# A row softmax on one core: part of a load moved to the store queue, and scaling row by row

## The chip, the cores and the metric

The kernel runs on one core of a Trainium2 chip. The time is that of the device, in microseconds, from the start to the end of one execution; lower is better. The core has several engines that work at the same time, each through its own list of instructions in order: VectorE (DVE), ScalarE (ACT), GpSimd (POOL) and SyncE (SP). TensorE (PE) has nothing to do here. Data goes between HBM and the on-chip memory SBUF through 16 DMA engines. A transfer is issued by SP, ScalarE or GpSimd; each of these has a queue of its own on the 16 engines (in the profile q1 is SP's, q10 is ScalarE's, q0 is GpSimd's).

## The reference

```python
def reference(x: np.ndarray) -> np.ndarray:      # x: 16 x 1024 x 512, float32
    temp = 0.5
    x_scaled = x / temp
    x_max = np.max(x_scaled, axis=-1, keepdims=True)
    exp_x = np.exp(x_scaled - x_max)
    return (exp_x / np.sum(exp_x, axis=-1, keepdims=True)).astype(np.float32)
```

It is a softmax over rows of 512 numbers, 16,384 rows. Input and output are 33.55 MB each.

## The kernel before

**Tiling.** The rows are cut into 8 chunks. A chunk is 128 partitions x 16 rows x 512 numbers, 4 MB; a partition holds 16 rows that follow each other in memory, so a whole chunk is 128 contiguous pieces of 32 KB. There are six buffers (`BUFS`), each for one chunk, and all work on a chunk is done in place: chunk 6 takes the buffer of chunk 0, chunk 7 that of chunk 1. `LOADS`, `BLOCKS` and `STORES` (L38 to L40) say in which groups of rows a chunk is loaded, worked on and stored. Chunk 0 is loaded as rows 0 to 3 and rows 4 to 15 and worked on in three blocks (4, 4 and 8 rows); chunks 1 to 6 are loaded and worked on whole; chunk 7 is loaded without its last row and worked on in two blocks of 8. Every chunk is stored whole. In all there are 11 blocks.

**The steps of a block.**

- `shift` (L71) issues the load of the chunk on SP when the chunk is new (L68), takes the maximum of each row, negated, on VectorE (L77, a reduce), and doubles it into a bias (L81).
- `exponentials` (L102) runs on ScalarE, one instruction for each row (L108): exp(2x + bias), with the sum of the row as a second result, which shows in the profile as an instruction of its own, ACTIVATION_READ_ACCUMULATOR.
- `scale_vector` (L120) takes the reciprocals of the sums on VectorE (L125) and multiplies seven eighths of the block's rows with them in one instruction (L127), whose second operand is the reciprocal spread over the row.
- `scale_scalar` (L133) multiplies the last eighth of the rows on ScalarE, one instruction for each (L138): two rows of 16, one of 8, none of 4.
- `store` (L144) issues the store of the whole chunk on ScalarE's queue behind the chunk's last block (L148).

**Order.** The order on each engine is that of the program text; a transfer or an instruction that needs another's result waits for it on its engine, and what stands behind it on that engine waits too. The loop over the blocks (L163) goes one block ahead with the exponentials and two ahead with the reduces:

```python
    exponentials(0, rows(0)[0])
    for i in range(n):
        if i + 1 < n:
            exponentials(i + 1, rows(i + 1)[0])
        scale_vector(i)
        scale_scalar(i)
        if i + 2 < n:
            shift(i + 2)
        store(i)
        if i + 1 < n:
            exponentials(i + 1, rows(i + 1)[1])
```

`rows` (L157) splits a block's exponentials into a part ahead of the store and a part behind it. Only chunk 1 has a second part, its last two rows (L159): the store of chunk 0 is issued after 14 of the 16 exponentials of chunk 1.

**Transfers.** SP issues the loads of chunks 0 to 5 at the start, without waiting. Its load of chunk 6 waits for the store of chunk 0 to land, that of chunk 7 for the store of chunk 1. The last row of chunk 7 is loaded by GpSimd (`load_last_row`, L88), in small pieces, after the eleventh exponential of chunk 5 has given the sign (L116). ScalarE's queue carries the eight stores and nothing else.

Of the kernel before, what the change touches and what calls it, by code (L numbers as in the profile page):

```python
# [1 line left out]

# [4 lines left out]


@with_exitstack
def kernel(  # L10
    ctx: ExitStack,
    tc: tile.TileContext,
    x: bass.AP,
    out: bass.AP,
):
    nc = tc.nc
    fp32 = mybir.dt.float32
    P = nc.NUM_PARTITIONS
    AX = mybir.AxisListType.X
    EXP = mybir.ActivationFunctionType.Exp  # L20
    COPY = mybir.ActivationFunctionType.Copy
    MAX = mybir.AluOpType.max

    D = x.shape[-1]
    xf = x.flatten_outer_dims()
    of = out.flatten_outer_dims()
    N = xf.shape[0]

    G = 16
    C = N // (P * G)
    assert C * P * G == N
    xr = xf.rearrange("(c p g) d -> c p g d", p=P, g=G)
    outr = of.rearrange("(c p g) d -> c p g d", p=P, g=G)
    WHOLE = [(0, G)]
    LOADS = [[(0, 4), (4, G)]] + [WHOLE] * 6 + [[(0, G - 1)]]  # L38
    BLOCKS = [[(0, 4), (4, 8), (8, G)]] + [WHOLE] * 6 + [[(0, 8), (8, G)]]
    STORES = [WHOLE] * 8  # L40
    BMAX = 16
    BUFS = 6

    data = ctx.enter_context(tc.tile_pool(name="data", bufs=BUFS))
    stats = ctx.enter_context(tc.tile_pool(name="stats", bufs=6))

    ctx.enter_context(tc.manual_schedule())


    warm = stats.tile([P, 1], fp32, name="warm", bufs=1)  # L50
    nc.vector.memset(warm, 0.0)  # L51
    nc.scalar.activation(out=warm, in_=warm, func=EXP)  # L52

    chunks = {}
    blocks = [(c, lo, hi) for c in range(C) for lo, hi in BLOCKS[c]]
    n = len(blocks)
    biases, sums, recips = {}, {}, {}

    finished = []

    def load(c):
        if c < BUFS:
            chunks[c] = data.tile([P, G, D], fp32, name="xt")
        else:
            chunks[c] = chunks[c - BUFS]
        xt = chunks[c]
        for lo, hi in LOADS[c]:
            part = nc.sync.dma_start(out=xt[:, lo:hi, :], in_=xr[c][:, lo:hi, :])  # L68
            finished.append(part.ins.name)

    def shift(i):  # L71
        c, lo, hi = blocks[i]
        if c not in chunks:
            load(c)
        b = hi - lo
        negmax = stats.tile([P, BMAX], fp32, name="negmax")
        nc.vector.tensor_reduce(  # L77
            negmax[:, 0:b], chunks[c][:, lo:hi, :], axis=AX, op=MAX, negate=True
        )
        biases[i] = stats.tile([P, BMAX], fp32, name="bias")  # L80
        nc.vector.tensor_scalar_mul(biases[i][:, 0:b], negmax[:, 0:b], 2.0)  # L81

    def load_last_row(signal):  # L88
        seen = stats.tile([P, 1], fp32, name="seen", bufs=1)
        copied = nc.gpsimd.tensor_copy(out=seen, in_=signal)  # L90
        finished.append(copied.ins.name)
        c = C - 1
        halves = "p (h d) -> p h d"
        to = chunks[c - BUFS][:, G - 1, :].rearrange(halves, h=2)
        of_ = xr[c][:, G - 1, :].rearrange(halves, h=2)
        for p0, p1 in ((P - 2, P), (0, P - 2)):
            part = nc.gpsimd.dma_start(  # L97
                out=to[p0:p1], in_=of_[p0:p1], max_dma_last_dim=2 * D
            )
            finished.append(part.ins.name)  # L100

    def exponentials(i, rows):  # L102
        c, lo, hi = blocks[i]
        if i not in sums:
            sums[i] = stats.tile([P, BMAX], fp32, name="sums")
        for g in rows:
            row = chunks[c][:, lo + g, :]
            nc.scalar.activation(  # L108
                out=row,
                in_=row,  # L110
                func=EXP,
                bias=biases[i][:, g : g + 1],
                scale=2.0,
                accum_out=sums[i][:, g : g + 1],
            )
            if c == BUFS - 1 and g == 10:  # L116
                load_last_row(sums[i][:, g : g + 1])


    def scale_vector(i):  # L120
        c, lo, hi = blocks[i]
        b = hi - lo
        k = b - b // 8
        recips[i] = stats.tile([P, BMAX], fp32, name="recip")
        nc.vector.reciprocal(recips[i][:, 0:b], sums[i][:, 0:b])  # L125
        rows = chunks[c][:, lo : lo + k, :]
        last = nc.vector.tensor_mul(  # L127
            rows, rows, recips[i][:, 0:k].unsqueeze(2).broadcast_to((P, k, D))
        )
        if i == n - 1:  # L130
            finished.append(last.ins.name)

    def scale_scalar(i):  # L133
        c, lo, hi = blocks[i]
        b = hi - lo
        for g in range(b - b // 8, b):
            row = chunks[c][:, lo + g, :]
            last = nc.scalar.activation(  # L138
                out=row, in_=row, func=COPY, scale=recips[i][:, g : g + 1]
            )  # L140
            if i == n - 1:
                finished.append(last.ins.name)

    def store(i):  # L144
        c, _, end = blocks[i]
        for lo, hi in STORES[c]:
            if hi == end:
                part = nc.scalar.dma_start(  # L148
                    out=outr[c][:, lo:hi, :], in_=chunks[c][:, lo:hi, :]
                )  # L150
                if c < C - 1:
                    finished.append(part.ins.name)

    shift(0)
    shift(1)

    def rows(i):  # L157
        c, lo, hi = blocks[i]
        cut = hi - lo - (2 if c == 1 else 0)  # L159
        return range(cut), range(cut, hi - lo)  # L160

    exponentials(0, rows(0)[0])
    for i in range(n):  # L163
        if i + 1 < n:
            exponentials(i + 1, rows(i + 1)[0])
        scale_vector(i)
        scale_scalar(i)
        if i + 2 < n:
            shift(i + 2)
        store(i)  # L170
        if i + 1 < n:
            exponentials(i + 1, rows(i + 1)[1])

    seen = nc.sync.nop()
    info = mybir.DependencyInfo(
        mybir.DependencyClass.Sync, mybir.DependencyReason.DATA
    )
    for name in finished:
        tc.add_manual_dep(seen.ins, name, info, reason="leaves one wait for the end")


# [1 line left out]
_INS = ['x']  # L183
_OUTS = [((16, 1024, 512), 'float32')]


# [23 lines left out]
```

## Time and profile before

| | us |
|---|---|
| median of 3 runs | 161.81 (161.65 to 161.95) |
| span of the profiled execution | 160.5 |
| VectorE busy | 134.6 |
| of it reduces (L77), 11 | 69.9 |
| of it broadcast multiplies (L127), 11 | 62.0 |
| ScalarE busy | 102.2 |
| of it exponentials (L108), 128 | 90.4 |
| of it row multiplies (L138), 15 | 9.9 |
| SP's load of chunk 6 issued | 68.67 |
| SP's load of chunk 7 issued | 88.02 |

The span goes from the first to the last instruction of the profiled execution; what lies between it and the median is launch and end. On the profile's page each engine has a row of 40 digits, one for each fortieth of the span (4.0 us here), 9 meaning 90% busy or more; the row DMA is the mean busy share of the 16 DMA engines. The chain is followed back from the last instruction, at each step to what released it. In the list of instructions by form a line gives the code line, the engine, the operation, what it writes and reads with shapes, the count, then the busy time and the mean ns of one. In the timeline a line gives the start in us, the duration in us, and the instruction. In the table of windows a line gives the stretch and its length, the busy time of DVE, ACT and POOL in it, the granted TensorE clock, the busy share of the DMA engines, and the GB/s that they moved. In the list of queues a line gives packets, MB, and the time of the packets as a share of 16 engines' time.

### The profile page before, as it was taken

The numbers are of one execution on the slowest core, as the hardware profiler recorded it, in microseconds if no ns is written. First come the engines' busy times: TensorE is split into PE (matmuls) and PEld (weight loads), VectorE is DVE, ScalarE is ACT, GpSimd is POOL, SyncE is SP. The second block draws the span as 40 slices with busy tenths as digits, with TensorE's granted clock in tenths as the row PEclk, the third lists the DMA queues.
The fourth block names the chain that finished last, engine by engine and source line by source line (L and its number), as shares of the span: only waits on it lengthen the run. The fifth ranks groups of instructions, "written<-read, shape, count | busy, mean of one in ns | idle before, by whom it ended". The sixth has DMA issues, their size and how long they took to land.

```text
span 160.5 us, 411 instructions
## 1 busy us (share of the span) xinstructions
DVE 134.6 (84%) x45; ACT 102.2 (64%) x273; POOL 1.9 (1%) x7
## 2 busy tenths in 40 slices
DVE  0607999999999999999999999999999999957000
ACT  3071549069989963998199909991899891790000
POOL 0000000000000000000000000030000000000000
DMA  5999999999989999999999999989999999999994
GB/s 184 470 408 498 400 392 457 457 392 402 506 269 425 490 392 400 506 400 392 490 425 392 474 434 392 490 383 483 422 450 400 400 465 441 392 457 449 400 441 204
DMA packets 2578, 67.13 MB, mean 418 GB/s; under 512 B 328, under 2 KB 328, under 8 KB 400
## 3 DMA queue, kind: packets, MB, share of 16 engines
q1 hardware_dynamic: 1296, 33.29, 49.3%
q10 hardware_dynamic: 1152, 33.55, 48.4%
q0 software_dynamic: 128, 0.26, 0.4%
q14 instruction: 2, 0.02, 0.0%
HBM read 33.55 MB, written 33.55 MB: 418 GB/s over the span
## 4 chain that ended last, share of the span: by engine, by line
DVE 75%; DMA 7%; issue 5%; ACT 3%; SPq 0%
DVE negmax L77 42%; DVE xt L127 31%; DMA xt<-in_x_dram 7%; ACT xt L108 3%; DVE bias L81 1%; DVE recip L125 1%; SPq L68 0%
## 5 line engine op out<-in xcount | busy, mean ns | idle before, releaser
L108 ACT ACTIVATE xt<-xt,bias 128x512 f32<-128x512 f32 x128 | 90.4, 708 | 41.5 <-DVE bias L81 40.6
L77 DVE TENSOR_REDUCE negmax<-xt 128x16 f32<-128x8192 f32 (+2 forms) x11 | 69.9, 6352 | 9.4 <-DMA xt<-in_x_dram 9.4
L127 DVE TENSOR_TENSOR xt<-xt,recip 128x7168 f32<-128x7168 f32 (+2 forms) x11 | 62.0, 5637 | 0.4
L108 ACT ACTIVATION_READ_ACCUMULATOR xt<-xt,bias 128x1 f32 x128 | 23.9, 187 | 0.0
L138 ACT ACTIVATE xt<-xt,recip 128x512 f32<-128x512 f32 x15 | 9.9, 706 | 0.0
L125 DVE RECIPROCAL recip<-sums 128x16 f32<-128x16 f32 (+2 forms) x11 | 2.4, 218 | 1.8 <-ACT xt L108 1.8
L81 DVE TENSOR_SCALAR bias<-negmax 128x16 f32<-128x16 f32 (+2 forms) x11 | 1.9, 173 | 0.4
L52 ACT ACT_TABLE_LOAD x1 | 1.3, 1283 | 0.7 <-PEq L194 0.7
L97 POOL DMA_DIRECT2D xt<-in_x_dram x2 | 1.5, 741 | 0.5 <-issue 0.5
L90 POOL COPY seen<-sums 128x1 f32<-128x1 f32 x1 | 0.2, 184 | 103.6 <-ACT xt L108 103.6
L51 DVE MEMSET warm<- 128x1 f32 x1 | 0.1, 59 | 0.8 <-PEq L194 0.8
L52 ACT ACTIVATE warm<-warm 128x1 f32<-128x1 f32 x1 | 0.2, 202 | 0.0
L194 POOL MEMSET const-float32-0.0<- 128x1 f32 x1 | 0.1, 93 | 0.2 <-issue 0.2
L194 POOL MEMSET const-bfloat16-1.0<- 128x1 bf16 x1 | 0.1, 95 | 0.0
L194 POOL MEMSET const-uint8-127<- 128x1 uint8 x1 | 0.1, 95 | 0.0
L194 POOL MEMSET const-float32-1.0<- 128x1 f32 x1 | 0.1, 93 | 0.0
## 6 DMA issues: line engine op xcount, KB each, us to landing
out_dram<-xt ACTq DMA_DIRECT2D x8, 4096.0 KB, 23.1
xt<-in_x_dram SPq DMA_DIRECT2D x6, 4096.0 KB, 34.8
xt<-in_x_dram SPq DMA_DIRECT2D x1, 3840.0 KB, 27.8
xt<-in_x_dram SPq DMA_DIRECT2D x1, 3072.0 KB, 11.6
xt<-in_x_dram SPq DMA_DIRECT2D x1, 1024.0 KB, 4.8
xt<-in_x_dram POOLq DMA_DIRECT2D x1, 252.0 KB, 15.4
xt<-in_x_dram POOLq DMA_DIRECT2D x1, 4.0 KB, 9.1
```

The costliest lines, as they stand in the source:

```text
L51: nc.vector.memset(warm, 0.0)
L52: nc.scalar.activation(out=warm, in_=warm, func=EXP)
L77: nc.vector.tensor_reduce(negmax[:, 0:b], chunks[c][:, lo:hi, :], axis=AX, op=MAX, negate=True)
L81: nc.vector.tensor_scalar_mul(biases[i][:, 0:b], negmax[:, 0:b], 2.0)
L90: copied = nc.gpsimd.tensor_copy(out=seen, in_=signal)
L97: part = nc.gpsimd.dma_start(out=to[p0:p1], in_=of_[p0:p1], max_dma_last_dim=2 * D)
L108: nc.scalar.activation(out=row, in_=row, func=EXP, bias=biases[i][:, g : g + 1], scale=2.0, accum_out=sums[i][:, g : g + 1],)
L125: nc.vector.reciprocal(recips[i][:, 0:b], sums[i][:, 0:b])
L127: last = nc.vector.tensor_mul(rows, rows, recips[i][:, 0:k].unsqueeze(2).broadcast_to((P, k, D)))
L138: last = nc.scalar.activation(out=row, in_=row, func=COPY, scale=recips[i][:, g : g + 1])
L194: nc = _bacc.Bacc("TRN2", target_bir_lowering=False, num_devices=1)
```

## The change

Three edits.

1. Chunk 5's load is split. Its first ten rows are loaded by ScalarE, on the queue of the stores, issued at the start behind the first small activation. `max_dma_last_dim` cuts this transfer into pieces of 1024 numbers, two rows, so that it has 5 pieces of 4 KB for each partition. Rows 10 to 15 are loaded by SP where the whole chunk was. In `shift` a load is now issued for a chunk's first block, whether or not the chunk already has a buffer.
2. The store of chunk 0 is issued behind all 16 exponentials of chunk 1.
3. VectorE scales all rows, one instruction for each row with the row's reciprocal as a scalar; ScalarE scales none.

```diff
-    LOADS = [[(0, 4), (4, G)]] + [WHOLE] * 6 + [[(0, G - 1)]]
+    SLOW = 10
+    LOADS = [[(0, 4), (4, G)]] + [WHOLE] * 4 + [[(SLOW, G)], WHOLE, [(0, G - 1)]]
...
     nc.scalar.activation(out=warm, in_=warm, func=EXP)
 
     chunks = {}
+    finished = []
+
+    def load_slowly(c):
+        chunks[c] = data.tile([P, G, D], fp32, name="xt")
+        part = nc.scalar.dma_start(
+            out=chunks[c][:, 0:SLOW, :],
+            in_=xr[c][:, 0:SLOW, :],
+            max_dma_last_dim=2 * 4 * D,
+        )
+        finished.append(part.ins.name)
+
+    load_slowly(BUFS - 1)
...
     def load(c):
-        if c < BUFS:
+        if c in chunks:
+            pass
+        elif c < BUFS:
             chunks[c] = data.tile([P, G, D], fp32, name="xt")
...
     def shift(i):
         c, lo, hi = blocks[i]
-        if c not in chunks:
+        if lo == 0:
             load(c)
...
-    def scale_vector(i):
+    def scale(i):
         c, lo, hi = blocks[i]
         b = hi - lo
-        k = b - b // 8
         recips[i] = stats.tile([P, BMAX], fp32, name="recip")
         nc.vector.reciprocal(recips[i][:, 0:b], sums[i][:, 0:b])
-        rows = chunks[c][:, lo : lo + k, :]
-        last = nc.vector.tensor_mul(
-            rows, rows, recips[i][:, 0:k].unsqueeze(2).broadcast_to((P, k, D))
-        )
+        for g in range(b):
+            row = chunks[c][:, lo + g, :]
+            last = nc.vector.tensor_scalar_mul(row, row, recips[i][:, g : g + 1])
...
-    def scale_scalar(i):
-        c, lo, hi = blocks[i]
-        b = hi - lo
-        for g in range(b - b // 8, b):
-            row = chunks[c][:, lo + g, :]
-            last = nc.scalar.activation(
-                out=row, in_=row, func=COPY, scale=recips[i][:, g : g + 1]
-            )
...
     def rows(i):
         c, lo, hi = blocks[i]
-        cut = hi - lo - (2 if c == 1 else 0)
+        cut = hi - lo
         return range(cut), range(cut, hi - lo)
...
-        scale_vector(i)
-        scale_scalar(i)
+        scale(i)
```

More of the change, by code (lines that the diff above doesn't have):

```diff
@@ L20 @@
     EXP = mybir.ActivationFunctionType.Exp
-    COPY = mybir.ActivationFunctionType.Copy
     MAX = mybir.AluOpType.max
@@ L57 @@
     biases, sums, recips = {}, {}, {}
-    finished = []
     def load(c):
-        if c < BUFS:
+        if c in chunks:
+            pass
+        elif c < BUFS:
             chunks[c] = data.tile([P, G, D], fp32, name="xt")
@@ L117, in exponentials @@
                 load_last_row(sums[i][:, g : g + 1])
-    def scale_vector(i):
+    def scale(i):
         c, lo, hi = blocks[i]
         b = hi - lo
-        k = b - b // 8
         recips[i] = stats.tile([P, BMAX], fp32, name="recip")
         nc.vector.reciprocal(recips[i][:, 0:b], sums[i][:, 0:b])
-        rows = chunks[c][:, lo : lo + k, :]
-        last = nc.vector.tensor_mul(
-            rows, rows, recips[i][:, 0:k].unsqueeze(2).broadcast_to((P, k, D))
-        )
+        for g in range(b):
+            row = chunks[c][:, lo + g, :]
+            last = nc.vector.tensor_scalar_mul(row, row, recips[i][:, g : g + 1])
         if i == n - 1:
             finished.append(last.ins.name)
-    def scale_scalar(i):
-        c, lo, hi = blocks[i]
-        b = hi - lo
-        for g in range(b - b // 8, b):
-            row = chunks[c][:, lo + g, :]
-            last = nc.scalar.activation(
-                out=row, in_=row, func=COPY, scale=recips[i][:, g : g + 1]
-            )
-            if i == n - 1:
-                finished.append(last.ins.name)
     def store(i):
```

## The prediction

> **What bounds the kernel now.** I read the page first (busy shares, the 40 slices, the chain), then equal windows of DMA throughput, then the stores, then single VectorE forms.
>
> ```profile
> span 160.5 us, 411 instructions
> DVE 134.6 (84%) x45; ACT 102.2 (64%) x273; POOL 1.9 (1%) x7
> ...
> DVE  0607999999999999999999999999999999957000
> ACT  3071549069989963998199909991899891790000
> ...
> DMA  5999999999989999999999999989999999999994
> ...
> HBM read 33.55 MB, written 33.55 MB: 418 GB/s over the span
> ...
> DVE 75%; DMA 7%; issue 5%; ACT 3%; SPq 0%
> ```
>
> The chain names VectorE with 75%, because VectorE works back to back. But the DMA row is at 9 from the second slice to the last but one, while VectorE stops four slices earlier. All 67.1 MB must pass the 16 DMA engines, and VectorE matters only where a store comes so late that they run dry. So I cut the busy stretch into windows of 9.7 us, in which 4 MB pass at full rate (4.19 MB / 432 GB/s):
>
> ```profile
> 4.50:14.20 9.70, 3.85 (x3) 2.93 (x8) 0.00 (x0) 1.00 1.03 444
> ...
> 33.60:43.30 9.70, 9.70 (x2) 9.70 (x28) 0.00 (x0) 1.00 1.01 433
> 43.30:53.00 9.70, 9.63 (x4) 8.98 (x26) 0.00 (x0) 1.00 0.99 378
> 53.00:62.70 9.70, 9.68 (x2) 5.92 (x16) 0.00 (x0) 1.00 1.00 432
> 62.70:72.40 9.70, 9.65 (x4) 9.47 (x27) 0.00 (x0) 1.00 1.00 432
> ...
> 130.60:140.30 9.70, 9.63 (x5) 5.08 (x14) 0.00 (x0) 1.00 1.00 432
> ```
>
> The last column is GB/s. It is 432, with loads alone (to 43), with loads and stores (53 to 111) and with stores alone (after 121), so 432 is the ceiling. One window falls short: 378 of 432 over 9.7 us is 1.2 us in which nothing moved (packets are counted where they start, so 1.1 to 1.2). The queue behind it:
>
> ```profile
> 44.10 0.37 ACTq L148 DMA_DIRECT2D out_dram<-xt  x1
> ...
> 147.48 0.34 ACTq L148 DMA_DIRECT2D out_dram<-xt  x1
> ```
>
> The first line is the first store of the run and the first use of ScalarE's DMA queue; the hole begins some 2 us behind it. Every later store is issued while the one before is still moving (4 MB every 16.6 us, median 23.1 us to landing), and no later window has such a hole. The second line is the last store. It lands after 12.2 us, of which 9.7 are data, and the first load of 1 MB needs 4.8 us with 2.4 of data: 2.4 or 2.5 us is the fixed part, so this store hardly queued. VectorE's end (147.4) is thus only just early enough now, with a slack of about 1 us at most.
>
> **The change part by part.** The sum is made against the profiled span, 160.5 us; the runs' median is 161.81, so 1.3 us lie around it, which I keep.
>
> *The slow load.* SP's one load of chunk 5 becomes ScalarE's of ten rows in 4 KB pieces (5 pieces x 128 partitions = 640, 40 for each DMA engine) and SP's of six rows. ScalarE's issue costs 0.34 to 0.37 us for 128 pieces, so between 0.34 and 5 x 0.37 = 1.9 us for 640. It stands behind the table load (ends 2.02) and ahead of the first exponentials, which start at 8.05 after 5.81 us of idleness: hidden; without that cover it would be up to 1.9 us on ScalarE. How fast the pieces go is shown by the only small pieces of before:
>
> ```profile
> q10 hardware_dynamic: 190, 5.28, 76.4%
> q1 hardware_dynamic: 64, 1.47, 21.4%
> q0 software_dynamic: 128, 0.26, 4.2%
> ...
> xt<-in_x_dram POOLq DMA_DIRECT2D x1, 252.0 KB, 15.4
> ```
>
> These are queue lines of the window 106 to 122. GpSimd's 252 KB (four 4 KB turns for each engine) needed 15.4 us beside two queues of 30 and 32 KB pieces, whose turns take 1.14 and 1.21 us at 27 GB/s for one engine: 4 x 2.4 = 9.6 us plus start and landing. So a queue gets one piece in each turn. From about 2 or 3 us on, ScalarE's pieces therefore go one by one between SP's large ones. Each load of 128 pieces is 8 turns and gets longer by 8 x 0.15 = 1.2 us: chunk 0's second part lands at about 14.8 (before 12.8, where VectorE's reduce waited for it; 8 turns longer, and the first 1 MB some 5), and each chunk 9.7 + 1.2 us after the one ahead of it: chunk 1 at 25.7, 2 at 36.6, 3 at 47.5; the 40 pieces end between 48 and 53. No bytes are added. The pieces cost more each: q0 moved 0.26 MB in 4.2% of 16 engines x 16 us = 10.8 us, 24 GB/s for an engine; q10 5.28 MB in 195.6 us, 27 GB/s. 2.62 MB at 16 x 24.4 instead of 16 x 27 take 6.7 instead of 6.1 us: at most +0.65, at least 0. A part of q0's pieces is under 4 KB, so I take the middle, **+0.35 us**.
>
> In the changed order SP's six-row load waits for the slow load's landing (about 54). Behind it on SP are the loads of chunks 6 and 7, which wait for stores 0 and 1 anyway (issued at 68.67 and 88.02 before). SP's queue holds chunk 4 until about 62, so it doesn't run dry.
>
> *The first store* goes behind all 16 exponentials of chunk 1. Reduce of chunk 1 at 25.7 (it now waits for the landing) + 8.68 + 0.2, then 16 x 0.705: issued at 46 instead of 44.1, into a queue that still holds slow pieces. Its data start when these end, at 48 to 53 (before 48.4). Store 0 then lands at about 70, store 1 at 87: as before. Cost 0, because SP's queue keeps the engines full meanwhile.
>
> *The hole of 1.1 us* is what can be won. What it costs after the change can't be read, only bounded: 0 if it belongs to waking an idle queue, since ScalarE's queue is now woken at 2 to 3 us, inside the ramp in which the first 1 MB needs 4.8 us anyway, and isn't idle at 46; 1.1 if it comes with the first write to HBM, or if waking costs as much in the ramp. Nearest rows: GpSimd's queue was woken at 105 and its window shows 451 GB/s, no hole, which speaks for the write; SP's own waking (issue 0.74, 1 MB landed 5.5) shows a slow start, which speaks for waking. I take the gain, **-1.1 us**.
>
> *Rows.* VectorE drops 11 broadcast multiplies (62.0 us) for 128 multiplies of one row by a scalar, and takes the 15 rows of ScalarE (9.9 us there). The trace has this operation only in small:
>
> ```profile
> L81 DVE TENSOR_SCALAR bias<-negmax 128x16 f32<-128x16 f32 x6 | 1.0, 174 | 0.2
> ...
> L81 DVE TENSOR_SCALAR bias<-negmax 128x8 f32<-128x8 f32 x3 | 0.5, 171 | 0.1
> L81 DVE TENSOR_SCALAR bias<-negmax 128x4 f32<-128x4 f32 x2 | 0.3, 170 | 0.1
> ```
>
> 4 ns for 12 more elements, 0.33 ns each; the broadcast multiply has (7625 - 3892) / 3584 = 1.04. The operation behind a bias starts 0.08 us after it. So a row costs 0.08 + 496 x 0.33 = 0.25 us, or 0.60 at 1.04 ns. With the same operation as the nearest row I take 0.29 (for a reading of 5 ns): 37 us in all. VectorE's chain from 12.8 to 147.4 is 134.6 us, of which 61 are multiplies and 1.8 idle: 72 stay. Starting at 14.8, it could end at 14.8 + 72 + 128 x 0.29 = 124; in fact it waits for chunk 7 (landed at about 115), and then needs two reduces (8.8), biases and reciprocals (1.2), 24 rows (7.0) and 8 exponentials (5.7): 138. The last store is wanted at 148. Cost 0, cover 10 us; it is used up at a row price of (148 - 86.8) / 128 = 0.48 us.
>
> [...]
>
> [...]
>
> Sum: 160.5 + 0.35 - 1.1 = 159.75, or 161.81 - 0.75 = **161.1 us** as a median.
>
> **The rivals.**
> - *The hole stays* (first write, or it moves to 3 us where the engines are already full). For it: GpSimd's waking was free. 161.81 + 0.35 = 162.15, bounds 161.8 and 162.5. Chance 0.36.
> - *Slower: a row is dear.* Place: VectorE between 15 and 163 us. At 0.60 us a row its chain ends at 14.8 + 72 + 77 = 164 instead of 147.4, and the time is 161.8 + 16.4 = 178. It decides from 0.48 us on. Against it: the 4 ns. Chance 0.04.
> - *The load isn't slow*: ScalarE's queue takes many pieces in a turn, is empty by some 17 us and asleep again at 46. Chunk 0 comes up to 5 us later, which VectorE's cover takes; the hole is back: 162.15. Against it: the 15.4 us. Chance 0.06.
>
> **How the numbers follow.** The forecast has 0.54. Its own range is 160.7 (pieces free, hole 1.2) to 161.5. The range 160.7 to 162.4 takes in the rivals with the hole; the dear row is left out, and a few tenths on either side. A measurement tells about 0.2%, 0.32 us, from no change. 162.15 lies on that line, so the 0.42 of the two rivals with the hole are split: same 0.20, slower 0.22 + 0.04 = 0.26, faster 0.54.
>
> **What would show it.** All windows between 5 and 158 us at 430 or more and none at 378; stores' queue busy from 3 us without a break; rows at 0.25 to 0.35 us; VectorE idle ahead of chunk 7; last store issued near 138 and long to landing (20 us). I am wrong if a window near 46 still lacks 1 us, if one near 3 us lacks it instead, or if the last store is issued after 148.

## The result, and the profile after

The changed kernel takes 163.43 us (median of 4 executions, 163.21 to 163.57) against 161.88 us (161.65 to 161.96) for the kernel before in the same session. The ratio is 1.0093, with a 95% interval of 1.0079 to 1.0108: slower by 1.55 us, where 0.7 us less was forecast. The time lies above the whole range (160.7 to 162.4).

The lines of the changed kernel's page that answer to those shown of before: the span, the busy shares, the rows of 40 slices, the queues, the chain by engine, and the groups of instructions.

```profile
span 161.8 us, 509 instructions
DVE 124.5 (77%) x162; ACT 92.9 (57%) x258; POOL 1.9 (1%) x7
DVE  0504998999999999999999996999739999380000
ACT  3070729249979936992799099808992924900000
DMA  5999999999989999999999999989999999999990
q14 instruction: 3, 0.02, 0.0%
DMA 55%; DVE 24%; ACT 8%; issue 1%; SPq 1%; DVEq 0%
L89 DVE TENSOR_REDUCE negmax<-xt 128x16 f32<-128x8192 f32 (+2 forms) x11 | 69.9, 6355 | 16.4 <-DMA xt<-in_x_dram 16.4
L139 DVE TENSOR_SCALAR xt<-xt,recip 128x512 f32<-128x512 f32 x128 | 51.7, 481 | 0.4
```

VectorE is no longer what the chain follows: it had 75% of it and now has 24%, transfers have 55%. Its reduces wait 16.4 us for loads, where they waited 9.4 us before, as the same line of the page before shows:

```profile
L77 DVE TENSOR_REDUCE negmax<-xt 128x16 f32<-128x8192 f32 (+2 forms) x11 | 69.9, 6352 | 9.4 <-DMA xt<-in_x_dram 9.4
```

The DMA row is at 9 nearly everywhere and the last slice fell from 4 to 0, which looks like an earlier end of the data; the span is nevertheless 1.3 us longer. The same 9.7-us windows as before (stretch, length, busy time of DVE, ACT and POOL, granted TensorE clock, DMA share, GB/s) show the bulk of the transfers:

```profile
4.50:14.20 9.70, 2.46 (x2) 2.93 (x8) 0.00 (x0) 1.00 1.09 466
33.60:43.30 9.70, 9.63 (x12) 8.68 (x25) 0.00 (x0) 1.00 1.00 426
43.30:53.00 9.70, 9.63 (x19) 8.89 (x25) 0.00 (x0) 1.00 0.99 397
53.00:62.70 9.70, 9.63 (x6) 5.68 (x17) 0.00 (x0) 1.00 1.00 432
130.60:140.30 9.70, 8.36 (x13) 4.58 (x13) 0.00 (x0) 1.00 1.00 432
```

The window that had 378 GB/s has 397: the hole got smaller and didn't go. The 426 in the window ahead of it is put down to the small pieces, which cost more time for each byte (159 ns for 4 KB beside 1213 ns for 32 KB: 7.6 times the time for 8 times the bytes). The loss is at the other end. The last windows of the kernel before:

```profile
157.00:158.00 1.00, 0.00 (x0) 0.00 (x0) 0.00 (x0) 1.00 1.14 492
158.00:159.00 1.00, 0.00 (x0) 0.00 (x0) 0.00 (x0) 1.00 0.01 0
159.00:160.00 1.00, 0.00 (x0) 0.00 (x0) 0.00 (x0) 1.00 0.00 0
```

and those of the changed kernel:

```profile
157.00:158.00 1.00, 0.00 (x0) 0.00 (x0) 0.00 (x0) 1.00 0.99 426
158.00:159.00 1.00, 0.00 (x0) 0.00 (x0) 0.00 (x0) 1.00 0.16 66
159.00:160.00 1.00, 0.00 (x0) 0.00 (x0) 0.00 (x0) 1.00 0.15 66
160.00:161.00 1.00, 0.00 (x0) 0.00 (x0) 0.00 (x0) 1.00 0.00 0
```

A share of 0.15 is 2.4 of 16 engines, and 66 GB/s over 1 us is two pieces of 32 KB. So for up to two microseconds two DMA engines still work on their part of the last store while the other fourteen are done. No view prints one DMA engine by itself, but the trace's events have the landing of every engine's share. For the last store, in us:

```
          8th of 16   14th   last    last store issued   last minus 8th
before       159.28  159.41  159.68        147.48              0.40
after        158.77  159.37  160.89        145.03              2.12
```

The 8th engine (called the middle one from here on) ends 0.51 us **earlier** than before, the last one 1.21 us later, and the span is 1.28 us longer. What the change costs is in the engines' falling out of step.

The 0.51 us is not all the change's. In nearly all other runs an execution takes 1.78 to 1.79 us more than the span of its profile (2.06 in s1_split_load). By that the profile of the kernel before shows an execution of about 162.3 us (160.51 + 1.78, an estimate), some 0.4 us slower than its median. x4_late_store (below), whose one edit did nothing to the time, has a profile of 161.94 us: there the 8th engine ends at 159.01 and the last at 159.33. Beside that the changed kernel's middle engine is 0.24 us earlier and its last one 1.56 us later, about the 1.55 us between the medians.

### The profile page after: what moved, and what is told of

It reads as the page before. It is cut to its first block, busy times and chain, and to the rows that moved or that the text cites. A ratio compares the mean times of both kernels' runs of the same rounds, so it can differ in the third digit from the quotient of the medians.

```text
span 161.8 us, 509 instructions
## 1 busy us (share of the span) xinstructions
DVE 124.5 (77%) x162; ACT 92.9 (57%) x258; POOL 1.9 (1%) x7
## 4 chain that ended last, share of the span: by engine, by line
DMA 55%; DVE 24%; ACT 8%; issue 1%; SPq 1%; DVEq 0%
DMA xt<-in_x_dram 36%; DMA out_dram<-xt 20%; DVE negmax L89 16%; ACT xt L120 8%; DVE xt L139 8%; SPq L80 1%; DVE recip L136 0%; DVE bias L93 0%; DVEq L203 0%
## 5 line engine op out<-in xcount | busy, mean ns | idle before, releaser
L89 DVE TENSOR_REDUCE negmax<-xt 128x16 f32<-128x8192 f32 (+2 forms) x11 | 69.9, 6355 | 16.4 <-DMA xt<-in_x_dram 16.4
L139 DVE TENSOR_SCALAR xt<-xt,recip 128x512 f32<-128x512 f32 x128 | 51.7, 481 | 0.4
```

The costliest lines, as they stand in the source:

```text
L89: nc.vector.tensor_reduce(negmax[:, 0:b], chunks[c][:, lo:hi, :], axis=AX, op=MAX, negate=True)
L139: last = nc.vector.tensor_scalar_mul(row, row, recips[i][:, g : g + 1])
```

## The experiments

Three quantities are worked out from the trace in the same way for every run.

- *Lag.* An undisturbed piece (a packet of the profile) takes 8.4 ns + 0.0368 ns per byte on its engine (1213 ns for 32 KB, 159 ns for 4 KB, in every kernel here). The sum of this over all pieces done by a time t, divided by 16, is the work done; t minus it is the lag. The *hole* is the rise of the lag from 40 to 70 us, *dry* its rise from 140 to 156 us (engines without work while the last store isn't issued yet).
- *Work*: the whole sum, 155.58 us before. Smaller pieces raise it.
- *Spread*: landing of the last store's last share minus the 8th.

| | median us (range) | work | hole | last store issued | dry | spread |
|---|---|---|---|---|---|---|
| before (its profile) | 161.81 (161.65–161.95) | 155.58 | 1.01 | 147.48 | 0 | 0.40 |
| after | 163.43 (163.21–163.57) | 155.94 | 0.55 | 145.03 | 0 | 2.12 |
| x1_no_slow | 166.73 (164.28–167.09) | 155.60 | 1.10 | 150.68 | 1.7 | 2.33 |
| x2_slow_only | 163.27 (163.12–163.45) | 155.92 | 0.41 | 149.15 | 1.4 | 0.65 |
| x3_rows_only | 162.36 (162.17–162.84) | 155.60 | 0.73 | 147.09 | 0 | 0.73 |
| x4_late_store | 161.99 (161.75–162.36) | 155.58 | 1.04 | 147.49 | 0 | 0.32 |
| p1_tiny_store | 161.97 (161.83–162.25) | 155.66 | 0.86 | 147.59 | 0 | 0.53 |
| p2_tiny_load | 162.14 (161.86–162.85) | 155.66 | 0.69 | 147.47 | 0 | 0.48 |
| p3_early_store | 163.43 (163.32–163.75) | 155.94 | 0.70 | 144.80 | 0 | 1.63 |
| p4_after_again | 163.71 (163.61–163.80) | 155.94 | 0.42 | 144.98 | 0 | 2.19 |
| s1_split_load | 167.72 (165.34–168.60) | 155.65 | 0.78 | 154.14 | 5.1 | 0.09 |
| s2_split_parts | 176.41 (175.34–177.56) | 155.90 | 2.72 | 153.71 | 0 | 0.90 |
| s3_fewer_rows | 163.50 (162.80–163.65) | 155.94 | 0.78 | 149.00 | 0.8 | 0.11 |
| n1_rows_late | 163.17 (162.60–163.35) | 155.94 | 0.50 | 147.24 | 0 | 1.87 |
| n2_more_instr | 164.91 (164.90–164.92) | 155.60 | 0.72 | 151.18 | 2.2 | 0.10 |
| y1_all_slow | 162.88 (162.76–162.99) | 156.07 | 0.39 | 142.21 | 0 | 1.46 |
| y2_all_slow_bmul | 162.86 (162.77–162.94) | 156.05 | 0.38 | 149.04 | 1.2 | 0.10 |
| y3_all_slow_rows_late | 162.69 (161.99–162.76) | 156.07 | 0.18 | 147.35 | 0 | 0.53 |
| z1_y3_again | 162.57 (one) | 156.07 | 0.21 | 147.38 | 0 | 1.17 |
| z2_s3_again | 162.85 (one) | 155.94 | 0.50 | 149.07 | 1.1 | 0.10 |

Times are those of 1 to 10 executions; all but the first two columns are from the one profiled, so work, hole, dry and spread stand for a single execution each. The kernel before had medians of 161.81 to 162.10 in the same sessions. The executions of x1_no_slow and s1_split_load scatter by some 3 us; their fastest (164.28 and 165.34) are still slower than every one of the kernel before.

### Each part by itself

Two theories are weighed in the next four runs: theory A, that the slow load puts the engines out of step, and the other, that the rows on VectorE with their added instructions do. By the other x1_no_slow would still take 163.0 to 163.5, x2_slow_only about 161.6, and x3_rows_only 163.0 or more.

**x1_no_slow**: the changed kernel without the slow load.

```diff
-    LOADS = [[(0, 4), (4, G)]] + [WHOLE] * 4 + [[(SLOW, G)], WHOLE, [(0, G - 1)]]
+    LOADS = [[(0, 4), (4, G)]] + [WHOLE] * 6 + [[(0, G - 1)]]
...
-    load_slowly(BUFS - 1)
```

> The changed kernel with chunk 5 loaded whole by SP, so the rows on VectorE and the late first store remain. In the changed kernel's trace two of the 16 DMA engines finish the last store 1.6 us behind the other 14 (they lost it one by one around 79 to 85 us), and a hole of 0.55 us remains at the first store. Theory A, the slow load is what puts engines out of step: this kernel is at 161.5 to 161.9, with a hole of 1.1 us at the first store and all engines ending within 0.5 us. [...]

**x2_slow_only**: the kernel before with the slow load alone (the lines of the change that split chunk 5's load, nothing else).

> The kernel before with the slow load alone. Theory A: 163.0 to 163.5, two late engines at the end, and the hole at the first store about 0.5 us instead of 1.1. [...]

**x3_rows_only**: the kernel before with the single rows on VectorE alone.

```diff
-        scale_vector(i)
-        scale_scalar(i)
+        scale(i)
```

> The kernel before with VectorE scaling row by row alone. Theory A: 161.7 to 162.0, no change, since VectorE is not the bound. [...] A row should cost 0.40 us from start to start as in the changed kernel's trace.

**x4_late_store**: the kernel before with the first store behind all 16 exponentials of chunk 1.

```diff
-        cut = hi - lo - (2 if c == 1 else 0)
+        cut = hi - lo
```

> The kernel before with the first store behind all 16 exponentials of chunk 1 alone. Both theories: 161.7 to 162.1, the first store 1.4 us later and its hole moved with it, no more. If it is over 162.5, the late store is a cause of its own.

The late store alone does nothing (161.99): its hole is as large as before's, behind a store issued 1.4 us later (45.51). The rows alone cost about 0.5 us (162.36 against 161.88), between the two expectations (161.7 to 162.0, and 163.0 or more). The slow load alone is the worst single part, 163.27, and for a reason that the table names: chunk 0's second part lands at 14.4 instead of 12.8, with the broadcast multiplies VectorE works back to back from there, so the last store is issued at 149.15, and the 16 engines stand still in between. The windows of x2_slow_only show it:

```profile
146.00:149.50 3.50, 3.06 (x1) 0.12 (x1) 0.00 (x0) 1.00 0.67 290
149.50:151.50 2.00, 0.00 (x0) 0.00 (x0) 0.00 (x0) 1.00 1.23 524
```

0.67 of 3.5 us is 1.2 us without data. The parts aren't additive. x1_no_slow, both of the others without the slow load, was expected at 161.5 to 161.9 or at 163.0 to 163.5 and is slower than all three together: in its profile one engine falls to 5.6 us behind the middle one by 125 us (chunk 7 lands at 125.48 where the middle engine is done at 119.85), and the last store is issued at 150.68. So engines get out of step without any slow load too; why it is so much here wasn't followed up.

### The hole

**p1_tiny_store** and **p2_tiny_load**: the kernel before, with a store, or a load, of one number for each partition on ScalarE's queue at the start, so that the first store isn't the queue's first use.

```diff
+    early = nc.scalar.dma_start(out=outr[0][:, 0, 0:1], in_=warm)
```

```diff
+    probe = stats.tile([P, 1], fp32, name="probe", bufs=1)
+    early = nc.scalar.dma_start(out=probe, in_=xr[0][:, 0, 0:1])
```

> The kernel before with a store of one number for each partition at the very start on ScalarE's queue, into places that the first real store writes over. It asks what the hole of 1.1 us at the first store belongs to. If to the first write to HBM or to the first use of the queue: the hole moves to the start, where it falls into the ramp, and the time is about 1 us less, 160.8 to 161.2. If it belongs to the moment at which a stream of stores joins a full stream of loads: 161.7 to 162.0, with a window of 378 GB/s at 46 us as before.

> The kernel before with a load of one number for each partition at the very start on ScalarE's queue, into a place that nothing reads. First use of the queue: 160.8 to 161.2 and no hole at 46 us. First write or the joining of two streams: 161.7 to 162.0, hole as before.

**p3_early_store**: the changed kernel with the first store ahead of chunk 1's last two exponentials, as before. **p4_after_again**: the changed kernel, unchanged.

```diff
-        cut = hi - lo
+        cut = hi - lo - (2 if c == 1 else 0)
```

> The changed kernel with the first store ahead of the last two exponentials of chunk 1 again, so slow load and rows without the late store. If the late engines come with the slow load: 163.2 to 163.6 as the changed kernel. If rows and late store together bring them (166.7 without the slow load): about 161.5, that is 161.9 less 0.55 at the hole plus 0.3 for small pieces.

> The changed kernel once more, to see whether its late engines are the same in another execution. If they come from the kernel: again one or two engines that lose about a microsecond near 79 us, the last store's slowest engine 1.5 us or more behind the middle one, 163.2 to 163.6. If they are chance: all engines within 0.7 us at the end and a time near 161.9.

The window 43.30 to 53.00 of p1_tiny_store and, in the second fence, of p2_tiny_load:

```profile
43.30:53.00 9.70, 9.63 (x4) 8.98 (x26) 0.00 (x0) 1.00 1.02 399
```

```profile
43.30:53.00 9.70, 9.63 (x4) 8.97 (x26) 0.00 (x0) 1.00 1.03 409
```

With 0.86 and 0.69 us the hole is there, whether the queue was used before or not, and whether HBM was written before or not. All kernels in which the store queue is idle when the stores begin have 0.69 to 1.10; a difference between 0.7 and 1.0 is what two executions differ by, so these two runs don't show that waking counts for nothing, only that most of the hole stays without it. Ten slow rows leave 0.41 to 0.78, all of chunk 5 on the store queue (below) 0.18 to 0.39 (s2_split_parts, slower throughout, is left out here). What makes the hole stays open. It is smaller where the store queue already carries a load when the first store is issued, but the ranges touch, and how it works isn't shown: with ten slow rows in the changed kernel the last slow piece ended at 49.34 us and the data of the first store, issued at 41.80, began only at 51.62, and the hole lies between; with sixteen rows the store's data began at 61.1, while the last slow pieces were still moving.

p3_early_store (163.43) and the changed kernel agree: the place of the first store is worth nothing. p4_after_again repeats the size, though in it one engine alone, not two, is 2.19 us behind the middle one at the end. Three places make 2.1 of that: 0.38 us at 39.1, 0.53 at 53.1, and 1.21 at 79.1, where one store piece of 32 KB takes 2427 ns instead of 1213. In the first profile of the changed kernel two such pieces are stretched, by 0.83 us at 79.05 and 1.07 at 79.21.

### Why one engine falls behind

At two of the three places the profile shows something else at the same moment. The page's list of queues has a queue q14 of kind "instruction": by its kind it brings instructions, in packets of 8 KB. In the changed kernel each takes 0.31 us. The line of the kernel before:

```profile
q14 instruction: 2, 0.02, 0.0%
```

The changed kernel has three (its line is shown above): 98 more instructions on the page, at 38.9, 52.9 and 97.4 us. A packet is taken to be one engine's: between 52 and 54 us the one there has 1.0% of the time of 16 engines, 0.32 us of one. Where one ends, a large piece starts that is stretched by 0.38, 0.53 and 0.25 us (0.17 and 0.25 in the kernel before, at 38.1 and 97.4 us); it is taken to be on the same engine. x3_rows_only has the third too, at 49.2, with 0.53, and ends with a spread of 0.73 instead of 0.32 to 0.53; no other loss was found in its profile for the 0.5 us that it costs. The waits that the profile of the changed kernel lists name no fetch as what ended one (16.8 us of ScalarE's are put down to nothing that the profile shows). The pieces behind the fetches are stretched, there by 0.25 to 0.53 us, which the page doesn't speak of.

**s3_fewer_rows** (the changed kernel, one broadcast multiply for each block of chunks 0 to 3), **n1_rows_late** (the kernel before with the slow load, and single rows for chunks 6 and 7 only) and **n2_more_instr** (the kernel before with 108 memsets of one column on VectorE) move or add the third fetch.

```diff
+        if c < 4:
+            rows = chunks[c][:, lo:hi, :]
+            nc.vector.tensor_mul(
+                rows, rows, recips[i][:, 0:b].unsqueeze(2).broadcast_to((P, b, D))
+            )
+            return
```

```diff
-        scale_vector(i)
-        scale_scalar(i)
+        if blocks[i][0] >= 6:
+            scale_rows(i)
+        else:
+            scale_vector(i)
+            scale_scalar(i)
```

```diff
+    pad = stats.tile([P, 1], fp32, name="pad", bufs=1)
+    for _ in range(54):
+        nc.vector.memset(pad, 0.0)
...
+    for _ in range(54):
+        nc.vector.memset(pad, 0.0)
```

> The changed kernel with chunks 0 to 3 scaled by VectorE in one broadcast multiply for each block and row by row only from chunk 4 on. Kernels with 128 row multiplies fetch instructions three times during the run (8 KB each on one DMA engine, near 39, 53 and 97 us), the others twice, and the engine that is hit loses 0.53 us at 53. If that fetch is part of the late engine: it is gone from 53 us or comes later, and the time is 0.3 to 0.6 us below the changed kernel, 162.9 to 163.2. If not: 163.3 to 163.7.

> The kernel before with the slow load, and row-by-row scaling on VectorE for chunks 6 and 7 only; ScalarE keeps its rows up to chunk 5. With the slow load alone (163.3) the engines ran dry for 1.3 us because the last store was issued at 149.15. Here VectorE should be 2.4 us earlier at the end, the last store at about 147, and there are too few instructions for a third fetch. If running dry and the fetch are all that spoils the slow load: 161.5 to 161.8 (0.55 won at the hole, 0.3 for small pieces). If one engine still loses about 1.2 us near 79 us: 162.5 to 163.2, slowest engine of the last store over 1 us behind the middle one.

> The kernel before with 108 tiny VectorE instructions more (a memset of one number for each partition, read by nobody) in VectorE's idle time before 12.8 us, so no transfer, no order and no scaling changes. Theory: more instructions mean one more fetch of 8 KB on one DMA engine, which that engine never makes up: a third packet on the instruction queue before 15 us, and 162.1 to 162.4. If the fetch costs nothing, 161.7 to 162.0.

The fetch goes where the instructions are: to 107.4 us in s3_fewer_rows, 142.6 in n1_rows_late, 10.4 in n2_more_instr, each time with 0.35 to 0.55 us on one engine (n1_rows_late was expected to have none). n2_more_instr, meant to show the price of a fetch by itself, says nothing on it: a memset takes 0.12 us from start to start, so the 108 don't fit into VectorE's idle time, the last store goes out at 151.18 and the engines are dry for 2.2 us. That the third fetch is the price of the rows is thus the likeliest reading, not shown by itself. s3_fewer_rows (163.50) has no loss near 79 us in its profile and ends together, but its profiled execution is also its fastest (162.80, the other three 163.40 to 163.65), and the broadcast multiplies bring the dryness back (last store at 149.00, 0.8 us). n1_rows_late is the cleaner one: the last store is issued at 147.24 and the engines aren't dry, the fetch near 53 us is gone, and the kernel still takes 163.17. The end of n1_rows_late in windows:

```profile
157.00:158.00 1.00, 0.00 (x0) 0.00 (x0) 0.00 (x0) 1.00 1.14 492
158.00:159.00 1.00, 0.00 (x0) 0.00 (x0) 0.00 (x0) 1.00 0.01 0
159.00:160.00 1.00, 0.00 (x0) 0.00 (x0) 0.00 (x0) 1.00 0.08 33
```

33 GB/s over 1 us is one piece of 32 KB: a single engine works on a microsecond after the others. It lost 1.18 us at 79.0, as in the changed kernel.

**s1_split_load** and **s2_split_parts** were to change what lies at 79 us, where SP's short pieces of chunk 5 (12 KB) meet chunk 6's large ones: SP alone loads chunk 5 in two parts (rows 0 to 9 and 10 to 15) in the kernel before, or ScalarE takes 80 whole partitions instead of ten rows of all 128 in the changed one.

```diff
-    LOADS = [[(0, 4), (4, G)]] + [WHOLE] * 6 + [[(0, G - 1)]]
+    LOADS = [[(0, 4), (4, G)]] + [WHOLE] * 4 + [[(0, 10), (10, G)], WHOLE, [(0, G - 1)]]
```

```diff
-    SLOW = 10
-    LOADS = [[(0, 4), (4, G)]] + [WHOLE] * 4 + [[(SLOW, G)], WHOLE, [(0, G - 1)]]
+    SLOW = 80
+    LOADS = [[(0, 4), (4, G)]] + [WHOLE] * 6 + [[(0, G - 1)]]
...
-            out=chunks[c][:, 0:SLOW, :],
-            in_=xr[c][:, 0:SLOW, :],
+            out=chunks[c][0:SLOW],
+            in_=xr[c][0:SLOW],
...
-            part = nc.sync.dma_start(out=xt[:, lo:hi, :], in_=xr[c][:, lo:hi, :])
+            p0 = SLOW if c == BUFS - 1 else 0
+            part = nc.sync.dma_start(out=xt[p0:P, lo:hi, :], in_=xr[c][p0:P, lo:hi, :])
```

> The kernel before with chunk 5 loaded by SP in two transfers, rows 0 to 9 and 10 to 15, so the short pieces of 12 KB are there and the slow load is not. In all four runs with the slow load one DMA engine, already 0.4 to 0.9 us behind, lost another 1 us (0.8 to 1.3) near 79 to 84 us, where the short pieces end and chunk 6 begins. If the short pieces beside 32 KB stores do it: one engine loses about 1 us near 76 us, the last store's slowest engine is over 1 us behind the middle one, 162.6 to 163.2. If the slow load is needed: 161.8 to 162.1, as before.

> The changed kernel with chunk 5 split by partitions instead of rows: ScalarE loads partitions 0 to 79 in the same 640 pieces of 4 KB, SP the other 48 in pieces of 32 KB, so the slow load is there and the short pieces are not. If the short pieces do it: no loss near 79 us, slowest engine about 0.9 us behind at the end (instruction fetches alone), 162.2 to 162.5. If the slow load does it: 163.2 to 163.7 as the changed kernel.

Both changed too much besides. In s1_split_load the stores are read to get more of each turn while the short pieces pass; chunk 7 lands at 127.1 instead of 115.8, and the last store is issued at 154.14: one engine did lose 1.10 us (at 86.1), but 5.1 us of dryness hide what it costs. In s2_split_parts the 128 partitions are loaded as 80 and 48, and everything is slower from the first microseconds on. Its first windows, where the changed kernel has 466 and 429 GB/s:

```profile
4.50:14.20 9.70, 2.46 (x2) 2.93 (x8) 0.00 (x0) 1.00 1.04 359
14.20:23.90 9.70, 6.47 (x8) 2.93 (x8) 0.00 (x0) 1.00 0.99 358
```

So neither tells anything of the seam. The next three take SP's short pieces away: all 16 rows of chunk 5 go through the store queue, and SP's queue is empty from 60 us until store 0 has landed. **y1_all_slow** does this to the changed kernel, **y2_all_slow_bmul** to x2_slow_only, **y3_all_slow_rows_late** to n1_rows_late.

```diff
-    SLOW = 10
-    LOADS = [[(0, 4), (4, G)]] + [WHOLE] * 4 + [[(SLOW, G)], WHOLE, [(0, G - 1)]]
+    SLOW = 16
+    LOADS = [[(0, 4), (4, G)]] + [WHOLE] * 4 + [[], WHOLE, [(0, G - 1)]]
```

> The whole of chunk 5 (16 rows, 64 pieces of 4 KB for each engine) goes through ScalarE's queue, and SP has no six-row load: its queue goes from chunk 4 (large pieces) to nothing at about 60 us, and to chunk 6 when store 0 has landed (about 75 us). Theory (one engine loses about 1.2 us where SP's 12 KB pieces meet chunk 6's large ones): there is no such seam, so no engine falls over 0.9 us behind the middle one between 60 and 100 us, and the last landing is less than 0.8 us behind the median one; small pieces cost +0.5 (0.30 x 16/10), the rest as in the changed kernel: 163.4 - 1.2 + 0.2 = 162.4 (162.0 to 162.8). Rival (the loss comes with the start of chunk 6's load or with the stores themselves, whatever was in front): one engine again falls 1 us or more behind near the start of chunk 6, and the time is 163.6 (163.2 to 164.0).

> The same load with the broadcast multiplies, ScalarE's row multiplies and the early store of the kernel before. Theory: no seam and no third instruction fetch, so the engines stay together (last landing less than 0.5 us behind the median one) unless the last store is again issued after 148 us, as it was with ten slow rows (149.15, which left the engines dry for 1.28 us): 161.81 + 0.5 - 0.6 = 161.7 if it is issued by 148, 163.0 if at 149. Rival (loss with the start of chunk 6): over 1 us on one engine near it, 163.3 or more.

> All of chunk 5 on the store queue with broadcast multiplies for chunks 0 to 5 and single rows for chunks 6 and 7 only, which ends VectorE some 2 us earlier. With ten slow rows the same step moved the last store from 149.15 to 147.24; here from 149.04 to about 147.1, so the 16 engines no longer run dry at 150 (1.1 us). Theory (the end waits for the slowest engine, whatever made it slow): the middle engine ends at about 158.5 and the one that is 1.2 to 1.5 us behind since about 61 us at 159.8 or later, so the time is 161.8 (161.4 to 162.3) and the last landing again stands over 1 us behind the median one. Rival (the engines' being out of step is only a matter of which queue's packet each takes first, and evens out by the end): the last landing is within 0.5 us of the median one, and the time is 162.86 - 1.1 - 0.4 = 161.3, which would beat the kernel before.

The seam isn't needed for the loss. In y1_all_slow and y2_all_slow_bmul the last engine is already 1.24 to 1.44 us behind the 14th of 16 when the slow load lands (63.35 and 63.16 against 61.9), 10 us ahead of chunk 6's load and without a 12 KB piece in the kernel. In y2_all_slow_bmul nothing is added near 79 us: the last engine is 1.45 us behind the middle one at 62 us and 1.44 at 149. So the loss moved with the small pieces: with ten slow rows it comes where SP's 12 KB pieces end, with sixteen where ScalarE's 4 KB pieces end. Whether the end of a run of small pieces beside 32 KB ones makes it was not tested, and s3_fewer_rows and z2_s3_again (below) have the same pieces and no loss near 79 us in their profiles. Both theories gave a number that y1_all_slow missed (162.4 and 163.6; 162.88 measured). What it and the others with 16 slow rows did gain is the hole: 0.18 to 0.39 us. The window 53.00 to 62.70 of y3_all_slow_rows_late, in which its first stores begin, and its neighbours:

```profile
43.30:53.00 9.70, 9.63 (x4) 8.97 (x25) 0.00 (x0) 1.00 0.99 422
53.00:62.70 9.70, 9.70 (x2) 7.67 (x22) 0.00 (x0) 1.00 1.01 419
62.70:72.40 9.70, 9.63 (x5) 7.72 (x22) 0.00 (x0) 1.00 1.00 432
```

The four executions of y3_all_slow_rows_late took 161.99, 162.63, 162.75 and 162.76 us. The profile fell on the first, and in it the engines are in step. That made a test possible: profile the same kernel once more.

**z1_y3_again** and **z2_s3_again**: y3_all_slow_rows_late and s3_fewer_rows, unchanged.

> The kernel with all of chunk 5 on the store queue and single rows for chunks 6 and 7, unchanged. Its four executions took 161.99 (the profiled one, in which the 16 engines end within 0.5 us of the middle one) and 162.63 to 162.76. Theory (the 0.7 us between them is one engine that falls behind near the end of the slow load): if this execution takes 162.6 to 162.8, one engine's pieces of chunk 5 land over 1 us behind the middle one's (near 63 instead of 62.3) and its last store lands 1 us or more behind; if it takes 162.0, the engines are in step. Rival (the 0.7 us come from elsewhere, such as the last store's issue or a hole): at 162.6 to 162.8 the engines are still within 0.6 us of each other.

> The changed kernel with one broadcast multiply for each of chunks 0 to 3, unchanged. Its four executions took 162.80 (the profiled one, with the engines in step at the end) and 163.40 to 163.65. Theory: at 163.4 or more one engine loses about 1.2 us near 79 us and ends 1 us or more behind; at 162.8 none does. Rival: at 163.4 or more the engines end within 0.6 us of each other.

z1_y3_again came out at 162.57. The last windows of y3_all_slow_rows_late, then those of z1_y3_again:

```profile
157.00:158.00 1.00, 0.00 (x0) 0.00 (x0) 0.00 (x0) 1.00 1.06 459
158.00:159.00 1.00, 0.00 (x0) 0.00 (x0) 0.00 (x0) 1.00 0.01 0
```

```profile
157.00:158.00 1.00, 0.00 (x0) 0.00 (x0) 0.00 (x0) 1.00 0.99 426
158.00:159.00 1.00, 0.00 (x0) 0.00 (x0) 0.00 (x0) 1.00 0.08 33
```

The same program with the same issue times (last store 147.35 and 147.38), the middle engine ending at the same time (158.78 and 158.72), and 0.58 us between the two times, as much as between their last landings:

```
                         slow load landed      last store landed
                         8th     last           8th      last      time
y3_all_slow_rows_late   61.70    62.27        158.78    159.31   161.99
z1_y3_again             61.74    62.81        158.72    159.89   162.57
```

One engine was 1.07 us behind at 62 us, and one is 1.17 behind at the end. The events don't name engines; that it is the same one, which kept its delay for 97 us, is read from the single late share in the stores between (1.07 at 71 us, 1.26 at 130 and 1.27 at 139). In these two runs the last share lands 0.53 and 1.17 us behind the middle one, and the price is 0.58 us in one and the same kernel. z2_s3_again took 162.85, like the profiled one of s3_fewer_rows (162.80), so what happens in those of 163.4 to 163.65 was not seen. It loses nothing near 79 us, as expected for such a time; one engine is 0.9 us behind at 149 us, but with the last store issued at 149.07 the engines are dry for 1.1 us, and it catches up in that time (spread 0.10).

No version beat the kernel before: y3_all_slow_rows_late in step equals it (161.99 beside 161.99 for the kernel before in that session), and in most executions it isn't in step.

## Why the prediction was wrong, point by point

- *What bounds the kernel*: the 16 DMA engines, as stated. Wrong was to treat them as one pipe of 432 GB/s, "so 432 is the ceiling", in which only windows below it cost time. **This is the step that failed: the sum 160.5 + 0.35 - 1.1 has no term for the engines' being out of step.** The spread at the end rose from 0.40 to 2.12 us, +1.72, or from 0.32, +1.80, against x4_late_store. With the middle engine that is -0.51 + 1.72 = +1.21 of the 1.28 us in the span, and -0.24 + 1.80 = +1.56 against x4_late_store. That the middle engine's 0.51 comes near the 0.75 of the sum says nothing for the sum: about half of it is that the profile of before shows an execution of about 162.3 us, and the sum's own two terms measure +0.36 - 0.46 = -0.10. For the same reason the "1.3 us around" the span are 1.78; the forecast as a difference isn't touched by it. The windows of the kernel before show an end at 0.01 share and no hint of a spread; the term couldn't be read there, only suspected from q14's two packets and from chunk 7's last share, which landed 1.8 us after the 8th. (VectorE stops three slices ahead of the transfers in the rows of 40, not four; nothing rests on it.)
- *The slow load*: right. Chunks landed at 14.5, 25.7, 36.8 and 48.3 (14.8, 25.7, 36.6 and 47.5 forecast), the pieces at 51.0 (48 to 53); the first piece moved at 4.4 us, not at 2 or 3; ScalarE's issue stood at 0.91, hidden. The pieces' extra work is 155.94 - 155.58 = 0.36 us (0.35).
- *The hole of 1.1 us*: mis-sized, and its mechanism not confirmed. 1.01 us became 0.55; 0.46 was won, not 1.1. With the hole alone put right the sum would still give about 161.7 us (161.81 + 0.36 - 0.46). That waking the queue makes it was not borne out (0.86 and 0.69 us stayed in p1_tiny_store and p2_tiny_load), nor the first write by itself.
- *The first store*: it was said to be issued at 46, behind the exponentials. It was issued at 41.80, with five exponentials still to start, as ScalarE's timeline shows (start, duration, instruction; ACTq is its issuing side):

```profile
41.69 0.70 ACT L120 ACTIVATE xt<-xt,bias 128x512 f32<-128x512 f32 x1
41.80 0.36 ACTq L147 DMA_DIRECT2D out_dram<-xt  x1
42.39 0.70 ACT L120 ACTIVATE xt<-xt,bias 128x512 f32<-128x512 f32 x1
```

  The store now waits for VectorE alone, while before it waited for ScalarE's own row multiply, which ended at 44.07. Without such a wait the issuing side ran ahead of the engine here. No harm: the store stood behind the slow pieces. Stores 0 and 1 landed at 69.64 and 85.65 (70 and 87).
- *Rows*: 0.40 us from start to start instead of 0.29 (bounds 0.25 to 0.60, threshold 0.48). VectorE's timeline, where four rows take 1.67 us:

```profile
16.93 0.17 DVE L136 RECIPROCAL recip<-sums 128x4 f32<-128x4 f32 x1
17.13 1.67 DVE L139 TENSOR_SCALAR xt<-xt,recip 128x512 f32<-128x512 f32 x4
18.73 4.41 DVE L89 TENSOR_REDUCE negmax<-xt 128x8 f32<-128x4096 f32 x1
```

  (18.73 - 17.13) / 4 = 0.40. The last store was issued at 145.03 instead of 138, so the cover was 3 us and not 10; it held, and cost 0. Most of these 7 us aren't the rows': 24 of them at 0.11 more make 2.6, and chunk 7 landed at 119.83, not at about 115. The rows' price came from elsewhere, most likely the third instruction fetch.
- *The rivals*: the hole that stays (162.15) and the dear row (178) named other mechanisms than the one that decided. The slower side was given as one cause on VectorE; the cause was in the DMA engines.

What the runs show of the 1.72 us: about 0.5 of it is most likely the third fetch (0.53 in the changed kernel, the same in x3_rows_only). About 1.2 is the loss of one engine, in some profiles of two, that comes with the slow load in most executions, near 79 us in the changed kernel, x2_slow_only, p4_after_again and n1_rows_late, at 84 in p3_early_store, near 62 with 16 slow rows. That it costs about its size at the end is shown by y3_all_slow_rows_late and z1_y3_again, one profiled execution of each kind. What makes that engine lose it is open: neither SP's short pieces nor the start of chunk 6's load is needed, and the program alone doesn't settle it, since the loss comes and goes between executions of one program. The slow load isn't the only way there either: x1_no_slow, without it, has an engine 5.6 us behind.

## What to carry to other kernels

In a kernel bound by DMA, the throughput by windows says how much moved, not who was last: look also at the last two microseconds for a share of 0.06 to 0.20, which is one to three of 16 engines that work alone. What one engine lost early stayed lost to the end here (1.07 us behind at 62 us and 1.17 at the end in z1_y3_again), unless all of them ran dry in between (0.9 us behind at 149 us, 1.1 us dry and 0.10 at the end in z2_s3_again). Count the instructions that a change adds: here 98 more on the page went with a third packet of 8 KB on the engines that move the data, and a piece behind it was stretched by 0.53 us. And when a load is stretched to keep a queue busy, price what starts later for it: here the slow load alone moved the last store from 147.5 to 149.2, and left the engines dry for 1.4 us.

## What the runs showed of the hardware that was not expected

- A queue's share went by its piece size: 40 pieces of 4 KB for each engine lasted from 4.4 to 49.3 us beside pieces of 24 and 32 KB. With 12 and 20 KB load pieces beside 32 KB store pieces, chunk 7 landed 11 us later (s1_split_load), which fits that, though no other run separates it.
- Splitting one chunk's load into 80 and 48 partitions slowed the whole kernel by 13 us (176.41 against 163.43), and from 5 us on, when ScalarE's 80 partitions were already being loaded but SP's 48 were far from their turn (359 GB/s instead of 466). SP's 32 KB pieces took 1428 ns instead of 1216 there (medians from 5 to 40 us). Why was not tested.
- A row of 512 numbers times a scalar of each partition takes 481 ns, 0.40 us from start to start; a memset of one column 59 ns, but 0.12 us from start to start.
- ScalarE's issuing side sent a store off at 41.80 us, 4 us ahead of the end of the exponentials that stand in front of it in the program.
